# Stored weight sums, one more seven-product group, three listings and a new ending in an eight-core decoder trunk

## The chip, the cores and the metric

One Trainium2 chip; the kernel runs on 8 cores, one sequence of 2048 tokens each, with no traffic between them. The metric is the device time of the slowest core, in microseconds. Some executions are slow: the cores of one die, or a pair of them, run at a lower granted TensorE clock (the share of its full speed that the trace shows as granted): in one run of before, of 2322.42 us, cores 4 to 7 had mean clocks of 0.807 to 0.813, the others 0.987 to 0.993. Runs that count as slow are kept out of all comparisons.

## The reference, cut to what matters

```python
c_act = silu(c)
for l in range(2):                                   # x: (8, 2048, 1024) float32
    mod = c_act @ w_mod[l] + b_mod[l]                # shift, scale, gate of three sub-layers
    h, gate = modulate(x, norm_g[l, 0], mod_f1)      # rmsnorm(x) * (1 + scale) + shift
    x = x + 0.5 * gate * swiglu(h, w_ffn_in[l, 0], w_ffn_out[l, 0])     # hidden width 2816
    h, gate = modulate(x, norm_g[l, 1], mod_mx)
    y = mixer_ab(h, ...) if l == 0 else mixer_pool(h, ...)
    x = x + gate * y
    h, gate = modulate(x, norm_g[l, 2], mod_f2)
    x = x + 0.5 * gate * swiglu(h, w_ffn_in[l, 1], w_ffn_out[l, 1])
return rmsnorm(x, final_g)
```

## The kernel before

Each SwiGLU is done in two passes of two 512-token tiles; I write F10p1 for layer 1, first SwiGLU ("first mixer" in the prediction), second pass. The 2816 hidden channels make 22 blocks: group 0 (12) and group 1 (10). A group is a gate stretch (28 products of 128 x 128 by 128 x 512 per block) and a down stretch. The products are done 2 x 2 with seven instead of eight block products. For that, VectorE forms four sums of a weight piece, and in the down stretch more sums of activations and more updates of X. A group is in `SEVEN` if its down projection is done so too.

```python
SEVEN = {(("F", l, i, p), g) for g in range(2) for l in range(2) for i in range(2) for p in range(2)
         if g == 0 or l == 0 or (l, i, p) == (1, 0, 0)}
KEEP = {}
...
def piece_sums(pc):                       # VectorE, 4 x 128x512 f16 per piece
    tt_(v(4), v(3), v(2), ALU.add, ...);      tt_(v(3), v(0), v(3), ALU.subtract, ...)
    tt_(v(5), v(4), v(0), ALU.subtract, ...); tt_(v(6), v(1), v(5), ALU.subtract, ...)
    if pc.keep is not None:               # there already, used by no piece
        add("sp", dma_start(out=sums_d[pc.keep], in_=SL[:, s, 1536:3584]), ...)
```

Weight pieces come by GpSimd's DMA into six slots (`SLOTS`). The modulation is made of 144 rows of 512 KB: SyncE loads a row into one of two `WMOD` buffers, VectorE multiplies it by the conditioning vector and adds up (1.22 us). Rows are mixed into the stream one at a time when VectorE has less than `SLACK` us of backlog.

```python
SLACK = 3
def slack():
    return Sd.tl["dve"].busy_after(Sd.tl["pe"].tail() - 0.5) < SLACK
def rows_pump():
    ...
    if row_tick[0] >= ROW_EVERY and rows_on[0] and slack():
        q = row_queue.pop(0); row_dot(q); row_prefetch()
def late_x():                             # tiles of the second pass, in F00p0's first down stretch
    for t in range(2, 4):
        for c in range(0, NC, 2):
            add("sp", dma_start(out=X[:, t, c:c + 2, :], in_=xT[t]...), ...)    # 512 KB
            yield
            yield
```

The pooling mixer is mixed into F10p1's group 1 and F11p0. The program is recorded with estimated costs and then "listed": each engine's order is made anew by due times. Orders are fixed when the program is built; every engine then works in its order (in the profile of after VectorE stands 4.07 us at the head of its order while TensorE needs what is behind).

```python
Sd.relist(("dve", "act", "pe"))           # once
...
rstd([3], True)                           # ending: statistic, Ln, Exp, then 8 chunks on VectorE
for c in range(NC):
    final_chunk(3, c)                     # two chunks per store
```

## Time and profile before

| | before |
|---|---|
| runs, us | 1938.27, 1973.97 (slow), 1936.89, 1937.07 |
| cores of the profiled run, us | 1927.7 to 1933.5, median 1930.8 |
| TensorE / VectorE busy, slowest core | 1880.4 / 1694.7 us |
| 20th real product starts | 68.7 us (median core) |
| start of the last product to the end | 13.3 us |

Two groups of VectorE work on the page of before (busy time, mean ns, then idle time ahead of the group and what ended most of it), which the change moves:

```profile
L465 DVE TENSOR_TENSOR SLOTS<-SLOTS 128x512 f16<-128x512 f16 x996 | 395.0, 417 | 17.0 <-DMA SLOTS<-win 10.3
...
L465 DVE SCALAR_TENSOR_TENSOR WMOD<-WMOD,CB 128x1024 f32<-128x1024 f32 x130 | 157.7, 1216 | 7.0 <-DMA WMOD<-wmod 6.9
```

The 996 weight sums cost 395 us of VectorE, and it waits 7 us for rows to land.

### The profile page before, as it was taken

The page shows a single profiled execution, that of the slowest core. Times are in us where ns is not written, and L with a number is a line of the kernel's source. Part 1 is how long each engine was busy: PE and PEld are TensorE (multiplying, and loading weights), DVE is VectorE, ACT ScalarE, POOL GpSimd, SP SyncE. Part 2 cuts the span into 40 slices and gives each one's busy share as a digit, 9 for nine tenths or more (in the row PEclk, how much of TensorE's full clock was granted, in tenths as well). Part 3 has the DMA queues.
Part 4 walks back from the last instruction along what each step waited for, and adds up shares of the span by engine and source line. Part 5 has one row for each costly group of instructions (what it writes and reads, how often), then busy time and mean ns, then how long its engine had stood idle before and what let it go on. Part 6 is the DMA issues. An engine that isn't in the chain of part 4 may idle for free.

```text
span 1933.5 us, 25425 instructions; the slowest of 8 cores (1927.7 to 1933.5 us)
## 1 busy us (share of the span) xinstructions
PE 1880.4 (97%) x8706; PEld 853.4 (44%) x8706; DVE 1694.7 (88%) x3256; ACT 1030.3 (53%) x1738; POOL 174.6 (9%) x330
## 2 busy tenths in 40 slices
PE   3999999999999999999999999999999999999997
PEld 1544444444444444444444444444444444444443
DVE  4897999999988999999988888888998899898865
ACT  3444754456454564555456554654556655664343
POOL 0000000001212000000000000000000000000000
PEclk9899999999999999999999999999999999999999
DMA  9799568797676686867664554555453545445752
GB/s 278 147 174 218 92 119 184 177 190 155 169 177 157 143 190 148 168 137 158 148 119 81 89 87 83 89 96 88 77 88 66 87 77 94 78 74 87 175 86 95
DMA packets 67517, 248.72 MB, mean 129 GB/s; under 512 B 7616, under 2 KB 7744, under 8 KB 67136
## 3 DMA queue, kind: packets, MB, share of 16 engines
q0 software_dynamic: 42192, 153.64, 47.6%
q1 hardware_dynamic: 25200, 93.45, 15.1%
q8 instruction: 74, 1.21, 0.2%
q14 instruction: 51, 0.42, 0.1%
HBM read 392.29 MB, written 8.39 MB: 207 GB/s over the span
## 4 chain that ended last, share of the span: by engine, by line
PE 88%; DMA 4%; DVE 3%; ACT 2%; SPq 1%; issue 1%; POOL 0%; DVEq 0%
PE ps L465 88%; DMA WMOD<-wmod 3%; DMA SLOTS<-win 1%; SPq L465 1%; DVE WMOD L465 1%; DVE SLOTS L465 1%; DVE ACTB L465 1%; DVE TP L465 1%; DVE X L465 0%; ACT ps L465 0%; ACT PMH L465 0%; DVE ps L465 0%; ACT ACTB L465 0%; ACT TP L465 0%; ACT L465 0%
## 5 line engine op out<-in xcount | busy, mean ns | idle before, releaser
L465 PE MATMUL ps<-H,SLOTS 128*128 128x512 f16 x5440 | 1199.7, 379 | 9.3 <-ACT ps L465 3.3
L465 PEld LDWEIGHTS ps<-H,SLOTS 128*128 128x128 f16 x5440 | 530.1, 98 | 657.5 <-issue 28.3
L465 ACT ACTIVATE ps<-ps 128x512 f32<-128x512 f32 x684 | 397.0, 582 | 567.8 <-PE ps L465 529.1
L465 PE MATMUL ps<-ACTB,SLOTS 128*128 128x512 f16 x2780 | 613.8, 379 | 0.1
L465 PEld LDWEIGHTS ps<-ACTB,SLOTS 128*128 128x128 f16 x2780 | 271.8, 98 | 328.4 <-issue 1.4
L465 DVE TENSOR_TENSOR SLOTS<-SLOTS 128x512 f16<-128x512 f16 x996 | 395.0, 417 | 17.0 <-DMA SLOTS<-win 10.3
L465 DVE SCALAR_TENSOR_TENSOR X<-ps,GH,X 128x512 f32<-128x512 f32 x424 | 307.7, 743 | 38.0 <-PE ps L465 34.8
L465 ACT ACTIVATE TP<-ps 128x512 f32<-128x512 f32 x400 | 237.9, 595 | 129.2 <-PE ps L465 126.1
L465 DVE TENSOR_TENSOR ACTB<-TP,ps 128x512 f16<-128x512 f32 x368 | 248.6, 683 | 36.2 <-PE ps L465 22.7
L465 ACT ACTIVATE SQ<-X 128x512 bf16<-128x512 f32 x224 | 131.0, 622 | 111.3 <-DVE X L465 53.6
L465 POOL DMA_DIRECT2D SLOTS<-win x176 | 93.0, 530 | 1032.5 <-PE ps L465 957.8
L465 DVE TENSOR_TENSOR TP<-ps,TP 128x512 f32<-128x512 f32 x176 | 121.0, 687 | 52.4 <-ACT ps L465 50.8
L465 DVE SCALAR_TENSOR_TENSOR WMOD<-WMOD,CB 128x1024 f32<-128x1024 f32 x130 | 157.7, 1216 | 7.0 <-DMA WMOD<-wmod 6.9
L465 DVE TENSOR_TENSOR TP<-X,RS 128x512 f32<-128x512 f32 x192 | 128.8, 686 | 8.1 <-ACT ACTB L465 5.0
L465 DVE TENSOR_TENSOR ps<-ps,TP 128x512 f32<-128x512 f32 x176 | 122.3, 695 | 12.6 <-PE ps L465 10.9
L465 DVE TENSOR_TENSOR ACTB<-ACTB 128x1024 f16<-128x1024 f16 (+1 forms) x188 | 104.3, 565 | 1.4
L465 POOL DMA_DIRECT2D SLOTS<-wout x88 | 46.4, 528 | 502.2 <-PE ps L465 502.2
L465 PE MATMUL ps<-SQ,ONES 128*128 128x512 bf16 x166 | 56.6, 427 | 29.4 <-ACT SQ L465 24.3
L465 ACT ACTIVATE H<-TP,MODT,AS 128x512 f16<-128x512 f32 x81 | 62.5, 805 | 20.3 <-DVE TP L465 13.6
L465 ACT ACTIVATE PMH<-TP,MODT,AS 128x512 f16<-128x512 f32 x60 | 47.5, 805 | 18.9 <-DVE TP L465 18.7
L465 ACT ACTIVATE ACTB<-TP,MODT,AS 128x512 f16<-128x512 f32 x51 | 40.6, 808 | 13.2 <-PE ps L465 7.0
L465 DVE TENSOR_TENSOR SQ<-SQ 128x1024 bf16<-128x1024 bf16 (+1 forms) x56 | 36.2, 647 | 10.5 <-ACT SQ L465 10.1
(74 smaller groups left out, 539.1 us busy)
## 6 DMA issues: line engine op xcount, KB each, us to landing
SLOTS<-win POOLq DMA_DIRECT2D x176, 512.0 KB, 5.7
WMOD<-wmod SPq DMA_DIRECT2D x131, 512.0 KB, 5.9
SLOTS<-wout POOLq DMA_DIRECT2D x88, 512.0 KB, 5.4
SLOTS<-wab POOLq DMA_DIRECT2D x28, 512.0 KB, 8.7
outT<-X SPq DMA_DIRECT2D x16, 512.0 KB, 3.3
ACTB<-wmod SPq DMA_DIRECT2D x13, 512.0 KB, 28.6
X<-xT SPq DMA_DIRECT2D x2, 2048.0 KB, 22.1
X<-xT SPq DMA_DIRECT2D x8, 512.0 KB, 9.7
```

Of the source, the lines that this page charges most:

```text
L465: return lambda E: getattr(E, name)(*a, **k)
```

## The change

The intent: with half of the sums of layer 1's first SwiGLU stored in the first pass and read back in the second, VectorE has room for the seven-product form in F10p1's group 1 as well, which takes 20 products off TensorE. Besides that: three listings, warming products placed as fillers wherever TensorE would be idle in the start, a smaller `SLACK`, and a new ending.

```diff
-WARM = 36
+WARM = 150
+PASSES = 3
-KEEP = {}
-SEVEN = {... or (l, i, p) == (1, 0, 0)}
+KEEP = {(1, 0): lambda g, part, n: n % 2 == 1}
+SEVEN = {... or (l, i, p) in ((1, 0, 0), (1, 0, 1))}
...                                        # listing: fillers have no due time and are dropped
...                                        # after the 20th real product; 51 of 150 remain
-    SLACK = 3
+    SLACK = 2.5
...
-    Sd.BW = 295e3                         # transfer rate assumed in the start
+    Sd.BW = 285e3
...                                        # the last two units: squares not added in pairs
-                    rstd([3], True)
-                    for c in range(NC):
-                        final_chunk(3, c)
+                    rstd([3], True, load=(0.0, 0.0), bank=0)       # Exp into PSUM
+                    act(RS[:, 1, :], PS[0][:], AF.Copy, [("ps", 0)], [("RS", 1)])
+                    for a, b, eng in ((3, 5, "dve"), (0, 2, "pool"), (5, 7, "dve"), (2, 3, "pool"), (7, 8, "dve")):
+                        final_part(3, a, b, eng)                   # VectorE reads PSUM, GpSimd reads RS
...
-    Sd.relist(("dve", "act", "pe"))
+    for _ in range(PASSES):
+        Sd.relist(("dve", "act", "pe"))
```

More of the change, by code (lines that the diff above doesn't have):

```diff
@@ L30, in keeps @@
     return KEEP.get(sub[1:], lambda g, part, n: False)(g, part, n)
-KEEP = {}
-SEVEN = {(("F", l, i, p), g) for g in range(2) for l in range(2) for i in range(2) for p in range(2) if g == 0 or l == 0 or (l, i, p) == (1, 0, 0)}
+KEEP = {(1, 0): lambda g, part, n: n % 2 == 1}
+SEVEN = {(("F", l, i, p), g) for g in range(2) for l in range(2) for i in range(2) for p in range(2) if g == 0 or l == 0 or (l, i, p) in ((1, 0, 0), (1, 0, 1))}
 SLW = 3584
@@ L41 @@
     __slots__ = ("idx", "eng", "fn", "deps", "semkey", "start", "end", "pos", "seq", "signal",
-                 "dma_target", "waits", "clock", "issue", "nbytes", "bw", "after", "then", "gate")
+                 "dma_target", "waits", "clock", "issue", "nbytes", "bw", "after", "then", "gate", "filler")
 class Timeline:
@@ L92, in __init__ @@
         self.wire = Timeline(False)
+        self.fill_to = None
     def key_free(self, k):
@@ L155, in add @@
         op.gate = set()
+        op.filler = 0
         op.start = t
@@ L180, in relist @@
         for o in ops:
-            if o.semkey is None:
+            if o.semkey is None and not o.filler:
                 cost.append(o.end - o.start)
@@ L184, in relist @@
                 cost.append(o.issue)
-            due.append(o.start + (0.0 if o.eng == "pe" else 8.0))
+            due.append(1e9 if o.filler else o.start + (0.0 if o.eng == "pe" else 8.0))
         succ = [[] for _ in ops]
@@ L195, in relist @@
                 left[o.idx] += 1
+                if q.filler:
+                    continue
                 gap = cost[d] if q.semkey is None else cost[d] + 3.5 + q.nbytes / self.BW
@@ L217, in relist @@
         wire = Timeline(False)
+        filling = True
+        stop = [o.idx for o in ops if o.eng == "pe" and self.fill_to is not None and o.idx >= self.fill_to][20:21]
         while events:
@@ L246, in relist @@
                 o.start = t
+                if x in stop:
+                    filling = False
+                if o.filler:
+                    o.filler = 1 if filling else 2
+                    cost[x] = o.issue if filling else 0.0
                 end = t + cost[x]
@@ L270, in emit @@
         by_eng = {e: [] for e in self.ENGS}
-        order = sorted(ops, key=lambda o: (o.start, o.idx))
+        order = sorted((o for o in ops if o.filler < 2), key=lambda o: (o.start, o.idx))
+        live = max((o for o in order if o.filler), key=lambda o: o.start)
         for o in order:
@@ L290, in emit @@
                 q = ops[d]
+                if q.filler == 2:
+                    q = live
                 if q.semkey is not None:
@@ L904, in stats_evac, with rstd @@
         act(RS[:, t % 2, :], PS[st["b"]][:], AF.Copy, [("ps", st["b"])], [("RS", t % 2)])
-    def rstd(ts, direct=False, after=0.0, load=(1.3, 1.3)):
+    def rstd(ts, direct=False, after=0.0, load=(1.3, 1.3), bank=None):
         srcs = {}
@@ L925, in rstd @@
         for i, t in enumerate(ts):
-            chain.append(add("act", I("activation", out=RS[:, t % 2, :], in_=RS[:, t % 2, :], func=AF.Exp, scale=-0.5),
-                             reads=[("RS", t % 2)], writes=[("RS", t % 2)], cost=0.75 + (load[1] if i == n - 1 else 0.0), after=at))
+            out, key = (RS[:, t % 2, :], ("RS", t % 2)) if bank is None else (PS[bank][:], ("ps", bank))
+            chain.append(add("act", I("activation", out=out, in_=RS[:, t % 2, :], func=AF.Exp, scale=-0.5),
+                             reads=[("RS", t % 2)], writes=[key], cost=0.75 + (load[1] if i == n - 1 else 0.0), after=at))
         chain[0].gate = set(table_ops)
@@ L1166, in part @@
                     self.w.done(dch // 2)
-                if self.last and dch % 2 == 1:
+                if self.last and n >= len(self.units) - 2:
+                    while self.sq:
+                        self.sq.pop(0)[0]()
+                    z = sq_rot.next()
+                    act(SQ[:, z, :], Xv(dch, 2 * self.p + tt), AF.Square, [Xk(dch, 2 * self.p + tt)], [("SQ", z)], src="sb")
+                    ones_mm(z, 2 * self.p + tt, NC // 2 + 1)
+                elif self.last and dch % 2 == 1:
                     self.flush_ones(NSQ // 2 - 1)
-                    self.sq.append((squares(dch - 1, 2 * self.p + tt, 2), 2 * self.p + tt))
+                    (q, at), t = squares(dch - 1, 2 * self.p + tt, 2), 2 * self.p + tt
+                    self.sq.append((lambda z=q[0], t=t: ones_mm(z, t, NC // 2 + tt), at))
         def flush_ones(self, most=NSQ // 2):
-            while self.sq and (len(self.sq) > most or self.sq[0][0][1] <= Sd.tl["pe"].tail()):
-                (q, _), t = self.sq.pop(0)
-                ones_mm(q[0], t)
+            while self.sq and (len(self.sq) > most or self.sq[0][1] <= Sd.tl["pe"].tail()):
+                self.sq.pop(0)[0]()
         def segments(self, tail):
@@ L1279, in final_chunk, with final_part @@
                 reads=[Xk(c - 1, t), Xk(c, t)], writes=[("OUT", t, c)], cost=0.06, dma=("OUT", t, c), nbytes=128 * 4096)
+    def final_part(t, a, b, eng):
+        for c in range(a, b):
+            if eng == "dve":
+                stt(Xv(c, t), Xv(c, t), SM[:, SM_FG + c:SM_FG + c + 1], PS[0][:], ALU.mult, ALU.mult,
+                    [Xk(c, t), "SM", ("ps", 0)], [Xk(c, t)])
+            else:
+                act(Xv(c, t), Xv(c, t), AF.Copy, [Xk(c, t), "SM"], [Xk(c, t)], src="sb", scale=SM[:, SM_FG + c:SM_FG + c + 1])
+                add("pool", I("tensor_tensor", out=Xv(c, t), in0=Xv(c, t), in1=RS[:, t % 2, :], op=ALU.mult),
+                    reads=[Xk(c, t), ("RS", t % 2)], writes=[Xk(c, t)], cost=c_pool(TT))
+        add("sp" if eng == "dve" else "act", I("dma_start", out=outT[t][:, a * TT:b * TT], in_=X[:, t, a:b, :]),
+            reads=[Xk(c, t) for c in range(a, b)], writes=[("OUT", t, c) for c in range(a, b)], cost=0.06, dma=("OUT", t, a),
+            nbytes=128 * 2048 * (b - a))
     BS = Af32[:, 40 * 256:42 * 256]
@@ L1575, in build_nc @@
     for n in range(WARM):
-        op = mm(PS[5][:], ONES[:], SQ[:, n % NSQ, :], True, True, [("SQ", n % NSQ), "ONES"], [("ps", 5)])
-        op.after = 28.0 + n * 0.6
-        op.start, op.end = op.after, op.after + op.issue
+        op = add("pe", I("matmul", PS[5][:], ONES[:], SQ[:, n % NSQ, :], start=True, stop=True, skip_group_check=True),
+                 reads=[("SQ", n % NSQ), "ONES"], writes=[("ps", 5)], cost=0.0)
+        op.issue, op.filler = c_pe(TT), 1
     tmp_rot.items = list(range(NTP))
@@ L1603, in build_nc @@
     Sd.BW = Sched.BW
+    Sd.fill_to = len(Sd.ops)
     for ph in PHASES:
@@ L1722, in build_nc @@
                         final_chunk(2, c)
-                    while dn.sq:
-                        (q, _), t = dn.sq.pop(0)
-                        ones_mm(q[0], t)
-                    rstd([3], True)
-                    for c in range(NC):
-                        final_chunk(3, c)
+                    rstd([3], True, load=(0.0, 0.0), bank=0)
+                    act(RS[:, 1, :], PS[0][:], AF.Copy, [("ps", 0)], [("RS", 1)])
+                    for a, b, eng in ((3, 5, "dve"), (0, 2, "pool"), (5, 7, "dve"), (2, 3, "pool"), (7, 8, "dve")):
+                        final_part(3, a, b, eng)
         else:
@@ L1738, in build_nc @@
         marks.append((sub, p, t_begin, Sd.tl["pe"].tail()))
-    add("sp", None, reads=[("OUT", t, c) for t in range(4) for c in (1, 3, 5, 7)], cost=0.01)
-    Sd.relist(("dve", "act", "pe"))
+    add("sp", None, reads=[("OUT", t, c) for t in range(4) for c in ((1, 3, 5, 7) if t < 3 else range(NC))], cost=0.01)
+    for _ in range(PASSES):
+        Sd.relist(("dve", "act", "pe"))
     with nc.Block() as block:
```

## The prediction

> **What bounds the kernel now.** I read the busy row of the page first, then the chain that ended last, then the TensorE timeline with its gaps, then windows of the stage that is changed, and last the beginning and the end of the span.
>
> ```profile
> PE 1880.4 (97%) x8706; PEld 853.4 (44%) x8706; DVE 1694.7 (88%) x3256; ACT 1030.3 (53%) x1738; POOL 174.6 (9%) x330
> PE 88%; DMA 4%; DVE 3%; ACT 2%; SPq 1%; issue 1%; POOL 0%; DVEq 0%
> ...
> 26.36 27.54 DMA WMOD<-wmod
> ...
> 1669.78 250.97 PE ps L465 x1162
> ```
>
> The last line is a stretch of the chain in which TensorE waits for nobody: 250.97 / 1162 = 0.216 us a product. That is the unit of account. The built program issues 8674 TensorE instructions before the change; less the 92 of the start, and less 64 short ones of 128 columns, some 8518 of them at 0.216 us make 1840 us. So about 95 us of the 1933.5 us span are something else: 62 us before the first real product, 13 us after the last one, and about 16 us of gaps and slow clock in between. Only those and the number of products can be gained.
>
> The gaps, from the TensorE timeline, are all small; after 70 us they sum to some 9 us, plus 1.84 us at the very end. The largest, and those in the changed stage:
>
> ```profile
> 188.35 1.02 PE L465 MATMUL ps<-H,SLOTS 128*128 128x512 f16 x4 [1.98 <-DVE TP L465]
> ...
> 1398.93 1.89 PE L465 MATMUL ps<-H,SLOTS 128*128 128x512 f16 x8 [0.24 <-ACT TP L465]
> 1452.33 1.02 PE L465 MATMUL ps<-H,SLOTS 128*128 128x512 f16 x4 [0.76 <-ACT ps L465]
> 1453.66 0.38 PE L465 MATMUL ps<-CB,WMOD 128*128 128x512 f16 x1 [0.31 <-DVE CB L465]
> ```
>
> Counting products places the second pass (p=1) of layer 1's first mixer at about 1281 to 1496 us. Its second hidden group (10 of the 22 blocks) starts near 1397, its plain down projection near 1458. The windows (busy of PE, PEld, DVE, ACT, POOL, then clock, DMA share, GB/s):
>
> ```profile
> 1280.00:1340.00 60.00, 60.00 (x279) 27.20 (x278) 48.97 (x95) 35.22 (x62) 5.29 (x10) 1.00 0.57 97
> 1340.00:1397.00 57.00, 57.00 (x265) 25.82 (x264) 52.75 (x107) 28.03 (x47) 4.57 (x9) 1.00 0.43 75
> 1397.00:1430.00 33.00, 32.76 (x152) 14.72 (x151) 31.57 (x62) 19.19 (x34) 2.81 (x6) 1.00 0.55 96
> 1430.00:1458.00 28.00, 26.77 (x122) 11.45 (x121) 27.76 (x56) 14.61 (x29) 2.11 (x4) 1.00 0.45 76
> 1458.00:1476.00 18.00, 18.00 (x85) 8.17 (x84) 12.46 (x21) 14.29 (x25) 1.59 (x3) 1.00 0.48 75
> 1476.00:1494.00 18.00, 18.00 (x85) 8.17 (x84) 17.88 (x32) 13.12 (x19) 1.06 (x2) 1.00 0.40 70
> ```
>
> From 1397 to 1458 VectorE is busy 59.3 of 61 us: the pooling mixer's vector work runs there beside the weight sums, and TensorE loses 1.3 us. Here VectorE is the second bound. DMA is not: 70 to 97 GB/s, where the first slice of the page shows 278.
>
> [...] after a 3.11 us gap at 45 to 48 us the clock granted from 50 to 60 us is 0.50, with TensorE busy 9.43 of 10. [...]
>
> **The change part by part.** Instruction counts are from the two built programs.
>
> 1. One more seven-product group. Second pass, layer 1, first mixer, group 1: the plain down projection has 16 units of 10 products, 160; the new one 4 x 7 x 5 = 140. Removed: 20 x 0.216 = 4.3 us of TensorE, on the path. It adds for VectorE 8 updates X<-ps,GH,X (24 instead of 16) at 745 ns, 12 activation sums (8 at 687, 4 at 418), and sums of 3 of the 5 output pieces, 12 at 418: 6.0 + 7.2 + 5.0 = 18 us quoted, some 15 us when overlaps are counted (two back to back take 0.75, not 0.84). ScalarE gets 12 copies at 0.58, 7 us; it has room (33.7 of 61).
>
> 2. Half of the sums kept. Odd pieces of all four lists: 6 + 3 of group 0, 5 + 2 of group 1, 16 pieces. 14 of them have sums in the second pass today: 14 x 4 = 56 instructions at 418 ns, 23 us quoted, leave VectorE; 36 in group 0 (13 us net of overlap) and 20 in group 1 (7 us). SyncE gets 16 stores and 16 loads of 512 KB. They add 16.8 MB to 249, and the loads of kept pieces fetch only three quarters of a piece. All of it lies at 1070 to 1496 us where DMA is half idle, 200 us between store and load: nothing on the path.
>
> Sum for this stage. VectorE: 193 busy of 215 us in the pass becomes about 193 - 20 + 15 = 188 of 211, but shifted: group 0 is relieved, group 1 gets 15 - 7 = 8 us more in 93 us, where it had 90 of 97. The order on VectorE shows the weight sums within the pooling stretch falling from 40 to 17, and the stretch behind it, before the next pass's H sums, growing from 57 to 74 instructions, where 5.5 us are idle today. I expect the 1.3 us of waits to go mostly (-1.0) and new short waits in the down projection to give 1.5 back. Stage: -4.3 - 1.0 + 1.5 = -3.8 us.
>
> 3. The start. The 36 fixed warming products become fillers placed wherever the order left TensorE idle; 51 remain. Before, fillers lie between the fp32 row products; now the rows run in one piece with 8 fillers between rows. Row 14 must still wait for its transfer (54.03 us), then row 15's 16 instructions take 3.55 us at half clock. Row 14 loses its interleaved fillers (5 x 0.43 = 2.1 us), but 8 fillers in front of it may hold it up by about 1, and 7 stand before the first real product. [...] I take -1.0, within -4 and +1.
>
> 4. The end:
>
> ```profile
> 1920.78 0.75 DVE L465 SCALAR_TENSOR_TENSOR X<-ps,GH,X 128x512 f32<-128x512 f32 x1 [0.32 <-PE ps L465]
> 1921.56 0.63 ACT L465 ACTIVATE SQ<-X 128x512 bf16<-128x512 f32 x1 [1.10 <-DVE X L465]
> 1922.22 0.42 DVE L465 TENSOR_TENSOR SQ<-SQ 128x512 bf16<-128x512 bf16 x1 [0.69 <-ACT SQ L465]
> ...
> 1923.21 0.69 ACT L465 ACTIVATE RS<-ps,EPSB 128x512 f32<-128x512 f32 x1 [1.02 <-PE ps L465]
> 1923.93 0.63 ACT L465 ACTIVATE RS<-RS 128x512 f32<-128x512 f32 x1
> 1924.59 5.39 DVE L465 SCALAR_TENSOR_TENSOR X<-X,SM,RS 128x512 f32<-128x512 f32 x8 [1.94 <-ACT RS L465]
> ```
>
> After the last update come square, pair sum, statistic, two activations, 8 chunks of 0.67 us and a store that lands 3.5 us later. The change drops the pair sum (0.45), and VectorE makes 5 chunks out of PSUM (about 3.4 us instead of 5.4). ScalarE copies the result (0.6) and GpSimd makes 3 chunks[...]. Last stores are 256 KB. From the update: 2.3 before the pair sum, 1.9 to the second activation's end, 0.6 copy[...] = 10.9, against 1933.5 - 1920.8 = 12.7: -1.8 us.
>
> 5. Three listings instead of one re-order all of TensorE, VectorE and ScalarE. The waits that cost most (table loads of 1.28 us, late rows near 180 us) stay, and the sequences differ in few rows elsewhere. I take -0.5, plus or minus 3.
>
> Sum: -3.8 - 1.0 - 1.8 - 0.5 = -7.1 us. The fast runs of before are 1936.9 and 1938.3; from 1937.6 this makes 1930.5. As listing is made to lessen the waits that remain, I shade it to 1930.
>
> **The rivals.** (a) VectorE becomes the bound in group 1: 98 us of work in 93. For it: 97% busy today and more work on balance. Against: the pooling stretch is what was full, and it is the one relieved. It would eat the 4.3 us: 1934. (b) Stores and loads on SyncE's in-order queue hold up modulation rows or slots: a store waits for VectorE's sums, rows queue behind it, a slot is free only when its store is done. For it: row transfers already hold things up at 180 us. Against: landing takes 5 to 6 us, a slot is held longer, 75 to 97 GB/s. It would cost 3 to 10 us: up to 1938. (c) The three listings remove most of the 9 us of gaps and the start gains 4: 1921. For it: the idle sums are real. Against: they come from delays that the listing doesn't foresee.
>
> **Range and chances.** The parts' errors (2 for the stage, 2 for the start, 3 for the lists, 1 for the end) add to about 4.5 us; 8 in 10 is 1923 to 1936. 2% is 39 us: faster by that would need more than all gaps, the slow clock and the ending together (16 + 13); slower by it, a stall in every pass. I give 0.01 and 0.01.
>
> **What would show it.** Right: 20 fewer ACTB,SLOTS products, 0.216 us each; the gaps at 1399 and 1452 gone; SLOTS sums falling from 996 to 952; the time from last update to end about 11 us; steady TensorE work starting no later than before (69.5 us). Wrong: new gaps before down products near 1460 released by VectorE (rival a); waits on SLOTS<-sums or longer WMOD rows at 1070 to 1490 us (b); fillers standing in front of a row that has landed[...].

The sum of the end came to 10.9 us after the last update, against 12.7, so -1.8: two of its terms are cut, GpSimd's three chunks, which were to end after VectorE's and so set the end, and the last store. The three that stand, 2.3 + 1.9 + 0.6, make 4.8 us. The forecast is -7.1 us in all, 1930.5 us, shaded to 1930.

## The result, and the profile after

| | before | after |
|---|---|---|
| runs, us | 1938.27, 1936.89, 1937.07 | 1933.84, 1933.57, 1931.71, 1937.72 |
| ratio of fast runs | | 0.9983 (0.9963 to 1.0004) |
| median core / slowest, profiled run | 1930.8 / 1933.5 | 1924.7 / 1932.2 |

A ratio is the mean time of one kernel's fast runs over that of the other's of the same rounds, so not quite the ratio of the medians. The point of 1930.0 was missed by 3.7 us, the range of 1923 to 1936 held the median of 1933.7 and three of the four runs. The interval of the ratio reaches over 1, so the 3.2 us between the mean times (1937.4 and 1934.2) are not clear of noise. The stages below are another matter: most of them agree within 0.03 us over the cores of a run, and where they don't the text says why.

The page of after, its busy row and the two VectorE groups:

```profile
PE 1881.2 (97%) x8702; PEld 853.2 (44%) x8702; DVE 1687.4 (87%) x3228; ACT 1035.1 (54%) x1754; POOL 176.7 (9%) x333
...
L480 DVE TENSOR_TENSOR SLOTS<-SLOTS 128x512 f16<-128x512 f16 x952 | 376.1, 418 | 12.6 <-DMA SLOTS<-win 7.6
...
L480 DVE SCALAR_TENSOR_TENSOR WMOD<-WMOD,CB 128x1024 f32<-128x1024 f32 x130 | 158.3, 1218 | 12.7 <-DMA WMOD<-wmod 12.7
```

The sums fell to 952 as predicted, and the wait for rows grew from 7.0 to 12.7 us on this core.

Where did the time go? I counted the products with weights in TensorE's timeline on each core and cut the span where the product of a fixed count starts (from the 6300th on the counts of kernels with the new group are 20 lower). The table has the median over the eight cores of each stage's length, so the rows don't add up exactly.

| stage | products | before | after |
|---|---|---|---|
| start | to 20 | 68.74 | 69.95 |
| F00p0 | 20 to 500 | 104.57 | 103.73 |
| F00p0 | 500 to 560 | 14.87 (max 18.6) | 16.72 (max 21.4) |
| F00p0 | 560 to 924 | 79.67 | 78.76 |
| F00p1 | 924 to 1848 | 201.74 | 201.22 |
| AB mixer, F01 | to 4592 | 604.8 | 604.8 |
| F10p0 | to 5516 | 202.47 | 201.34 |
| F10p1 group 0 | to 6020 | 112.23 | 112.24 |
| F10p1 group 1, gate | to 6300 | 68.34 | 67.77 |
| F10p1 group 1, down | to 6460 | 35.83 | 30.73 |
| F11p0 group 0 | to 6964 | 112.23 | 114.76 |
| F11p0 group 1 | to 7404 | 103.19 | 101.88 |
| F11p1 | to the last | 206.77 | 206.99 |
| last product to the end | | 13.26 | 12.97 |

The last product starts 5.7 us earlier on the median core (1917.4, then 1911.7). Three things stand out: the named group gains 5.7 us, the group behind it gives 2.5 back, and the slowest core gains far less than the median one. Windows of these three stages on the slowest core, first of before (core 3), then of after (core 7); columns as in the prediction:

```profile
1394.00:1462.33 68.33, 66.86 (x307) 29.49 (x306) 66.22 (x132) 39.05 (x71) 5.43 (x11) 1.00 0.47 80
1462.33:1498.17 35.84, 35.84 (x168) 16.26 (x167) 30.61 (x53) 25.34 (x39) 2.50 (x5) 1.00 0.45 74
1498.17:1610.40 112.23, 112.23 (x522) 50.87 (x521) 98.97 (x187) 60.57 (x104) 9.49 (x18) 1.00 0.49 83
```

```profile
1397.19:1464.96 67.77, 67.13 (x312) 30.17 (x311) 66.39 (x124) 43.05 (x79) 5.80 (x11) 1.00 0.55 111
1464.96:1495.69 30.73, 30.73 (x143) 13.80 (x142) 30.20 (x56) 23.20 (x37) 2.12 (x4) 1.00 0.39 70
1495.69:1610.45 114.76, 113.01 (x522) 50.57 (x520) 105.29 (x201) 64.05 (x109) 9.49 (x18) 1.00 0.49 84
```

In the two windows of group 1 TensorE is busy 102.70 us before and 97.86 after, and idle 1.47 and 0.64. But VectorE, which had 5.2 us free in the down stretch, is now busy 30.20 of its 30.73 us and takes a backlog into the next pass: 201 instructions instead of 187 there, and TensorE waits at its head. The gaps of TensorE in the timeline of after, core 7 (start, length, instructions; in brackets the idle time before them and what ended it):

```profile
1498.15 0.38 PE L480 MATMUL ps<-H,SLOTS 128*128 128x512 f16 x1 [0.35 <-ACT ps L480]
1500.83 2.67 PE L480 MATMUL ps<-H,SLOTS 128*128 128x512 f16 x10 [0.79 <-DVE H L480]
1504.05 1.02 PE L480 MATMUL ps<-H,SLOTS 128*128 128x512 f16 x4 [0.54 <-ACT ps L480]
```

These 1.68 us are most of the 2.5 given back. The gaps that the prediction showed at 1399 and 1452 us are gone.

Most of the spread of the cores comes from one place, products 500 to 560. The timeline of after, core 7, VectorE and TensorE:

```profile
190.47 1.23 DVE L480 SCALAR_TENSOR_TENSOR WMOD<-WMOD,CB 128x1024 f32<-128x1024 f32 x1 [4.07 <-DMA WMOD<-wmod]
...
192.45 3.69 PE L480 MATMUL ps<-H,SLOTS 128*128 128x512 f16 x8 [3.97 <-DVE TP L480]
```

VectorE stands 4.07 us at the head of its order, waiting for a modulation row that the AB mixer needs over 250 us later; behind it is what TensorE needs now. In this stage core 7 took 21.4 us, core 1 14.7. Of the 7.5 us by which core 7 stood over the median core, 4.7 come from here, 1.8 from F10p0 and 1.5 from the start. In F10p0 its VectorE waits for a row again, soon after SyncE issued two stores of sums, and TensorE loses 1.58 us behind it:

```profile
1097.76 1.23 DVE L480 SCALAR_TENSOR_TENSOR WMOD<-WMOD,CB 128x1024 f32<-128x1024 f32 x1 [2.99 <-DMA WMOD<-wmod]
```

Without stores, in before and in e2, F10p0 takes 202.46 to 202.48 us on every core; with them some 201.2 where no row is late, up to 203.13 in after and 206.88 in e1. So the late rows here come with the stores; no run tests that by itself. The slowest core stood 7.5, 4.9, 5.1 and 7.9 us over the median core in the four runs of after (6.3 on average), 2.7 in the profiled run of before and 2.3 to 6.8 in 22 other fast runs (4.7 on average).

### The profile page after: what moved, and what is told of

Its sections match the earlier page's. It is cut to its first block, busy times and chain, and to the rows that moved or that the text cites. A ratio compares the mean times of both kernels' runs of the same rounds, so it can differ in the third digit from the quotient of the medians.

```text
span 1932.2 us, 25507 instructions; the slowest of 8 cores (1921.1 to 1932.2 us)
## 1 busy us (share of the span) xinstructions
PE 1881.2 (97%) x8702; PEld 853.2 (44%) x8702; DVE 1687.4 (87%) x3228; ACT 1035.1 (54%) x1754; POOL 176.7 (9%) x333
## 4 chain that ended last, share of the span: by engine, by line
PE 91%; DMA 4%; DVE 2%; SPq 1%; ACT 1%; issue 0%
PE ps L480 91%; DMA WMOD<-wmod 4%; SPq L480 1%; DVE X L480 1%; DVE TP L480 0%; DVE WMOD L480 0%; DVE ACTB L480 0%; DVE SLOTS L480 0%; ACT SQ L480 0%; ACT ps L480 0%; ACT L480 0%; ACT H L480 0%; ACT TP L480 0%; ACT PMH L480 0%; ACT ACTB L480 0%
## 5 line engine op out<-in xcount | busy, mean ns | idle before, releaser
L480 ACT ACTIVATE ps<-ps 128x512 f32<-128x512 f32 x696 | 404.5, 582 | 585.1 <-PE ps L480 575.0
L480 DVE TENSOR_TENSOR SLOTS<-SLOTS 128x512 f16<-128x512 f16 x952 | 376.1, 418 | 12.6 <-DMA SLOTS<-win 7.6
L480 DVE SCALAR_TENSOR_TENSOR X<-ps,GH,X 128x512 f32<-128x512 f32 x432 | 312.8, 746 | 30.9 <-PE ps L480 26.1
L480 DVE SCALAR_TENSOR_TENSOR WMOD<-WMOD,CB 128x1024 f32<-128x1024 f32 x130 | 158.3, 1218 | 12.7 <-DMA WMOD<-wmod 12.7
L480 DVE TENSOR_TENSOR ACTB<-ACTB 128x1024 f16<-128x1024 f16 (+1 forms) x200 | 111.3, 567 | 1.2
L480 DVE TENSOR_TENSOR H<-H 128x1024 f16<-128x1024 f16 (+1 forms) x72 | 43.6, 624 | 2.1 <-ACT H L480 2.0
```

Of the source, the lines that this page charges most:

```text
L480: return lambda E: getattr(E, name)(*a, **k)
```

## The experiments

Twelve kernels ran, e1 to e12; all were correct. When I wrote the expectations I took the stage bounds wrongly from the counts: products 4976 to 5900 are called the first pass or F10p0 in them, and 5900 to 7000 "the stage". Really 5900 to 7000 is the end of F10p1's group 0, its group 1 and all of F11p0's group 0. The counts and the lengths are as stated, so the tests hold; this table has both, the true stages first (medians of eight cores, us).

| | before | after | e1 | e2 | e3 | e4 | e9 | e10 |
|---|---|---|---|---|---|---|---|---|
| F10p0 | 202.47 | 201.34 | 201.16 | 202.47 | 201.16 | 201.15 | 201.30 | 205.53 |
| F10p1 g1 gate | 68.34 | 67.77 | 71.76 | 64.55 | 67.34 | 69.37 | 71.15 | 67.34 |
| F10p1 g1 down | 35.83 | 30.73 | 35.96 | 41.21 | 34.53 | 36.24 | 30.22 | 30.22 |
| F11p0 g0 | 112.23 | 114.76 | 113.20 | 118.58 | 112.43 | 113.20 | 114.96 | 113.83 |
| F11p0 g1 | 103.19 | 101.88 | 103.20 | 101.88 | 101.88 | 101.87 | 103.30 | 101.88 |
| products 5900 to 6200 | 70.33 | 70.20 | 73.32 | 69.07 | 69.93 | 70.14 | 70.37 | 70.36 |
| products 6200 to 7000 | 182.33 | 179.32 | 183.87 | 191.64 | 180.64 | 184.93 | 183.79 | 177.28 |
| last product starts | 1917.4 | 1911.7 | 1919.9 | 1924.3 | 1914.8 | 1919.3 | 1918.9 | 1914.2 |

### e1_keepseven: the two named parts alone

```diff
-KEEP = {}                                 (in the kernel before)
+KEEP = {(1, 0): lambda g, part, n: n % 2 == 1}
-... or (l, i, p) == (1, 0, 0)}
+... or (l, i, p) in ((1, 0, 0), (1, 0, 1))}
```

> The kernel before with only the kept sums and the extra seven-product group; start, listing and ending as before. Stages are counted in products with the weight slots, per core. My theory (the stated change is worth its 20 products and the waits of that stage): from product 6200 to 7000 (20 fewer) 182.3 us becomes about 179.3, as in the changed kernel; the stages next to it (the first pass of this mixer, 202.5; products 7000 to 7924, 208.5) stay, as do the start (product 20 at 68.7) and the ending; the median core is 3 us shorter, ratio 0.998. Rival (the listings make the gain): 6200 to 7000 stays within 1 us of 182.3. Rival (stores and loads cost): the first pass, where stores are, grows above 202.5.

Measured: 1942.48 us, ratio 1.0013 (0.9995 to 1.0031). The three stages from F10p1's group 1 to F11p0's group 0 take 220.92 us, 216.40 before: 4.5 us longer with 20 products less; products 6200 to 7000 take 183.87 us, where I had expected 179.3. In the timeline of its slowest core TensorE waits four times in the down stretch, 5.1 us in all, like this:

```profile
1492.13 1.24 PE L465 MATMUL ps<-ACTB,SLOTS 128*128 128x512 f16 x5 [1.46 <-DVE X L465]
...
1498.95 3.40 PE L465 MATMUL ps<-ACTB,SLOTS 128*128 128x512 f16 x15 [1.86 <-ACT ps L465]
```

So the named parts alone, in the old listing, cost more in waits on VectorE than they save.

### e2_nokeep: after, without stored sums

```diff
-KEEP = {(1, 0): lambda g, part, n: n % 2 == 1}
+KEEP = {}
```

> The changed kernel with nothing kept: the second pass makes all its sums again, 64 more on VectorE, and there is no store or reload. If VectorE is the second bound there (my theory), products 6200 to 7000 take 181 to 185 us instead of 179.3, with gaps released by VectorE, and the kernel is 2 to 5 us slower than the changed one. If the kept sums only unload an engine that has room, 179.3 stays and the time with it. If the reloads cost something, this kernel is faster.

Measured: 1947.3 us, ratio 1.0036 (1.0018 to 1.0054). The three stages take 224.34 us, 11.1 more than in after (213.26), and VectorE is busy 41.20 of the 41.21 us of the down stretch. I had expected 181 to 185 us for products 6200 to 7000, and they take 191.64. The stored sums are what makes the group pay. They also shorten F10p0: 202.47 without, 201.15 to 201.34 with them in e1, e3, e4 and after; the two gaps of 0.32 and 0.67 us before 1200 us stand in e2 as in before.

### e3_noseven: after, without the new group

```diff
-... or (l, i, p) in ((1, 0, 0), (1, 0, 1))}
+... or (l, i, p) == (1, 0, 0)}
```

> The changed kernel with the old set of seven-product groups; sums are kept. My theory: products 6200 to 7000 (again 20 more) take 179.3 + 4.3, less the waits that come with the extra group (about 1.5): 182 to 183; the kernel is 2.5 to 4 us slower than the changed one. Rival (the group's gain is eaten by VectorE and the relief by kept sums gives the 3 us): 180 to 181 and the time equal within 1 us.

Measured: 1936.81 and 1933.43 us in two fast runs, two slow, so no ratio; the profile is of a fast run. The three stages take 214.30 us, against 213.26 with the group: it is worth 1.04 us, not 4.3. With plain products TensorE doesn't wait once in these stages on the slowest core; with seven it loses what the table shows at F11p0's head. Products 6200 to 7000 took 180.64 us; the rival's 180 to 181 was right, mine of 182 to 183 wrong.

### e4_onepass: after, listed once

```diff
-PASSES = 3
+PASSES = 1
```

> The changed kernel listed once instead of three times. If the listings made the gains outside the named stage, products 4976 to 5900 go back from 201.2 to 202.5, products 7000 to 7924 from 207.2 to 208.5, 560 to 700 from 30.4 to 31.3, and the median core is 3 to 4 us longer. If they come from the kept sums, the fillers or the smaller slack, these stages stay at 201.2, 207.2 and 30.4. The spread of the cores at products 500 to 560 should tell whether the order of the third listing or chance makes the late rows worse: 14.7 to 18 us here if it is the order, up to 21 as in the changed kernel if not.

Measured: 1939.42 us, ratio 1.0001 (0.9985 to 1.0017). The last product starts 7.6 us later than in after. The three stages take 218.81 us (5.6 more), F01p0 203.24 (201.73), the rest hardly changes. F10p0 stays at 201.15, where I had expected the listings to have made the gain; they didn't, the stored sums did (e2). Products 500 to 560 take up to 21.4 us here too, so it is not the order of the third listing that makes the rows late.

### e5_warm37: after, fewer fillers offered

```diff
-WARM = 150
+WARM = 37
```

> The changed kernel with 37 fillers instead of 150 offered: the 14 that stood behind row 15, in front of and among the first real products, are gone; those before the rows stay. My theory (fillers in front delay the first products, and with them the copy on ScalarE behind which the last H chunks wait): from the end of row 15 to product 20 it takes 9.3 us in the changed kernel and 6.8 before; here 6.5 to 7.5, product 20 at 67 to 68.5 instead of 70.0, and the whole kernel 1.5 to 2.5 us shorter on the median core. Rival (the last H chunks and their sums set the start anyway): product 100 stays at 87.3 within 0.5 and the time with it.

Measured: 1931.08 us, ratio 1.0001 (0.9948 to 1.0053); of its four runs one (1952.67) has a pair of cores at a granted clock of 0.971, and counts as fast; the other three are 1928.8 to 1932.9. The 20th product starts at 68.54 us (69.95 in after), as expected, and product 100 earlier too, so the rival is out. The median core of the profiled run ends at 1924.7 us, as in after, so the 1.5 to 2.5 us are not seen there; over the three undisturbed runs it ends at 1921.7 to 1924.7, in the four of after at 1924.7 to 1928.3. TensorE's timeline, after core 7, then e5 core 6:

```profile
61.78 3.15 PE L480 MATMUL ps<-SQ,ONES 128*128 128x512 bf16 x7
64.72 1.76 PE L480 MATMUL ps<-H,SLOTS 128*128 128x512 f16 x4
66.32 0.38 PE L480 MATMUL ps<-SQ,ONES 128*128 128x512 bf16 x1
```

```profile
61.27 0.59 PE L480 MATMUL ps<-SQ,ONES 128*128 128x512 bf16 x1 [0.40 <-DVE AS L480]
61.65 5.33 PE L480 MATMUL ps<-H,SLOTS 128*128 128x512 f16 x17
```

In after, seven fillers, at half clock still (0.50 granted from 61.78 to 64.72 us), stand in front of the first real product, and nine more among the next; in e5 one is left in front, and 17 products run in one piece behind it. From the end of row 15 to the first real product it takes 2.80 us in after, 0.78 in e5 and 0.24 in before, on every core.

### e6_hold: after, rows 24 to 31 held back and made up in group 1 of F00p0

```diff
+        held = 24 <= q < 32               # in row_dma: not before TensorE's work at this point
+            op.deps.add(max(o.idx for o in Sd.ops[-120:] if o.eng == "pe"))
-            if row_queue:
+            if row_queue and row_queue[0] < row_cap[0]:       # 24, lifted in group 1, rows on there
```

> The changed kernel with modulation rows 24 to 31, which are needed only by the next mixer, held back until the late X tiles are in. My theory (these rows land late behind the X tiles, VectorE waits for them in its order, and TensorE behind it; the slowest core of a run is the one hit hardest): products 500 to 560 take 14.7 to 15.5 us on every core instead of 14.7 to 21.4, the slowest core comes within 3 us of the median core instead of 5 to 8, and the kernel is 3 to 5 us faster than the changed one, about 1929 to 1930. Rival (weight pieces that land late do it): the spread at 500 to 560 stays above 3 us. Rival (the spread comes from elsewhere): 500 to 560 is even, the slowest core stays 5 us over the median.

Measured: three fast runs of 1933.25 to 1936.14 us, ratio 0.9987 (0.9972 to 1.0003). Products 500 to 560 take 14.7 to 15.4 us on all cores, and the slowest core stands 2.1 us over the median one in the profiled run (3.3 and 5.3 in the other two): the cause of this stage's spread is as thought, but not all of the cores' spread lies in this stage. And 560 to 924 grows from 78.76 to 83.91: the rows that were held now stand in the way of the next group. No net gain.

### e7_tail: after, a second Exp for the copy and smaller first pieces

```diff
-                    act(RS[:, 1, :], PS[0][:], AF.Copy, [("ps", 0)], [("RS", 1)])
-   ((3, 5, "dve"), (0, 2, "pool"), (5, 7, "dve"), (2, 3, "pool"), (7, 8, "dve"))
+                    act(RS[:, 1, :], RS[:, 1, :], AF.Exp, [("RS", 1)], [("RS", 1)], src="sb", scale=-0.5)
+   ((3, 4, "dve"), (0, 1, "pool"), (4, 6, "dve"), (1, 3, "pool"), (6, 8, "dve"))
```

> The changed kernel with the second activation made twice, into PSUM and into SBUF, so that VectorE need not wait for the copy, and with first pieces of one chunk. My theory (the end is the first store plus 2.1 MB at some 400 GB/s): VectorE starts its chunks 0.6 us after the first of the two activations ends instead of 1.2, the first store is ready 1.2 us sooner, and the time from the last product to the end falls from 13.0 to about 11.8 us. Rival (GpSimd's chunks set the end, as I predicted): it stays at 12.4 or more.

Measured: two fast runs, 1931.29 and 1930.37 us, ratio 0.9969 (0.9951 to 0.9987); last product to end 12.06 us instead of 12.97. The timelines of the ending, after core 7, then e7 core 0:

```profile
1922.42 0.60 ACT L480 ACTIVATE ps<-RS 128x512 f32<-128x512 f32 x1
1923.05 0.60 ACT L480 ACTIVATE RS<-ps 128x512 f32<-128x512 f32 x1
1923.68 3.88 DVE L480 SCALAR_TENSOR_TENSOR X<-X,SM,ps 128x512 f32<-128x512 f32 x5 [3.21 <-ACT RS L480]
1923.73 3.72 POOL L480 TENSOR_TENSOR X<-X,RS 128x512 f32<-128x512 f32 x3 [41.83 <-ACT RS L480]
```

```profile
1921.37 0.63 ACT L480 ACTIVATE RS<-RS 128x512 f32<-128x512 f32 x1
1921.37 3.88 DVE L480 SCALAR_TENSOR_TENSOR X<-X,SM,ps 128x512 f32<-128x512 f32 x5 [2.58 <-ACT ps L480]
1922.08 3.71 POOL L480 TENSOR_TENSOR X<-X,RS 128x512 f32<-128x512 f32 x3 [41.86 <-ACT RS L480]
```

In after VectorE waits for the copy as well (the copy ends at 1923.65 us, VectorE starts at 1923.68): both read the same PSUM bank, and the program orders the two readers; no run here tried without. With a second Exp from SBUF, VectorE starts as soon as the first is done (at 1921.37 us in e7, where the first ends at 1921.33). VectorE's five chunks take 3.88 us in both kernels, though GpSimd starts 0.05 us behind VectorE in after and 0.71 us behind it in e7: no slowing of VectorE by GpSimd shows here. The rest of after is bound by the stores: a window of its core 7 holds nothing but transfers.

```profile
1928.00:1930.00 2.00, 0.00 (x0) 0.00 (x0) 0.00 (x0) 0.00 (x0) 0.00 (x0) 0.50 1.02 401
```

In e7 it is no longer the stores alone. Its first store is issued 4.6 us after the last product starts, 6.0 in after: that is 1.4 us earlier, but the end comes only 0.9 earlier. Between the first pieces its DMA engines are partly idle, 0.70 busy from 1923 to 1924 us, and then (core 0):

```profile
1924.00:1925.00 1.00, 0.00 (x0) 0.00 (x0) 0.96 (x2) 0.00 (x0) 1.00 (x2) 0.50 0.74 281
```

So there the chunks hold the stores up again. What each of the two edits is worth alone no run shows.

### e8_hold6: after, six rows held until F00p1

```diff
-    row_cap = [24]                        (of e6)
+    row_cap = [26]                        # lifted at F00p1's start, no rows in group 1
```

> The hold again, on six rows alone (26 to 31, which were the ones that VectorE met while their loads stood behind the eight token tiles), let go at the start of the first mixer's second pass, and with no rows made up in the group between. Theory (the spread of the slowest core comes from VectorE waiting in order for rows that nobody needs yet): products 500 to 560 take 14.7 to 16 us on every core, products 700 to 924 take 48.35 again and not the 53.5 of the first hold, the slowest core stands at most 3.5 us over the median core, and the slowest core's span is 1925 to 1929 where the changed kernel had 1932.2. Rival (the spread is the cores' own, and only moves to another stage): slowest less median stays at 5 to 8 us with the excess in another stage, and the time stays at 1931 to 1934.

Measured: 1968.68 to 1980.93 us, ratio 1.0185 (1.0154 to 1.0216), "unclear" by the rule; all four runs count as fast, but have cores at a lower clock, so this ratio is not one of undisturbed runs. The stall is gone as expected (median 14.92; two cores at a lower clock took 17.8), and 560 to 924 is back at 78.74. But F00p1 takes 203.97 us and the first 80 products of the AB mixer 29.1 to 35.0 us, by core, instead of 17.3: the rows had become due, and the mixer waited. My expectation had VectorE's missing 7 us vanish in F00p1; VectorE has no such room. What follows on some cores is worse. Windows of e8, core 0 and then core 6:

```profile
500.00:550.00 50.00, 50.00 (x216) 21.90 (x215) 34.56 (x64) 15.39 (x27) 7.49 (x16) 0.81 0.57 123
```

```profile
70.00:150.00 80.00, 80.00 (x306) 33.10 (x305) 63.24 (x128) 31.94 (x56) 5.30 (x10) 0.81 0.58 115
```

After the pause core 0 (as 1, 2 and 3) was granted 0.81 of the clock from 500 to 650 us, core 5 all of it. Cores at a mean clock of 0.962 to 0.979 stand in all four runs of e8. That the pause sets this off is not shown: cores 6 and 7 of the same run, 6 the slowest of all, had 0.81 from 70 us on, long before it, and most kernels had such runs.

### e9_slack3: after, with the old SLACK

```diff
-    SLACK = 2.5
+    SLACK = 3
```

> The changed kernel with the one figure SLACK back at 3, with three listings. Theory (the small gains far from the named stage are SLACK's, since one listing kept most of them): products 560 to 700 take 31.1 to 31.3 us (30.41 with 2.5), products 7000 to 7924 take 208.2 to 208.5 (207.20), the first mixer's second pass 201.5 to 201.7 (201.22), in sum +1.5 to +2.6 us. Rival (the other start or the listings make them): these three stay within 0.2 us of the changed kernel's.

Measured: one run, 1939.63 us. Half a miss: 560 to 924 (78.74) and F00p1 (201.27) don't change, so that gain isn't SLACK's; F11p0's group 1 goes back to 103.30 as I thought. But the largest effect lies where I had not looked for it: F10p1's gate stretch takes 71.15 us (67.77), and the last product starts 7.2 us later. With the old SLACK the three named stages take 216.32 to 219.68 us, by core, median 217.89: they gain nothing on before (216.40).

### e10_keepall: after, all 33 eligible sums stored

```diff
-KEEP = {(1, 0): lambda g, part, n: n % 2 == 1}
+KEEP = {(1, 0): lambda g, part, n: True}
```

> All 33 eligible sums stored and reloaded instead of 16: 68 fewer sums of 0.39 us, about 27 us less of VectorE, in the second pass. Theory (with seven products in group 1 VectorE is what the stage waits for, and gave back 3.3 of the 4.3 us): the stage falls from 249.5 to 246 to 247 us, the first pass stays at 201.2, the median core ends 2.5 to 3.5 us earlier, 1921 to 1922. Rival (17 more stores and reloads of 0.5 MB meet SyncE's row loads or the weight loads): the first pass grows by over 1 us or the stage stays at 249 or over, with waits of TensorE or VectorE on DMA in either.

Measured: 1936.4 to 1937.1 us in three runs; a fourth, 1959.73, has a pair of cores at 0.979 but counts as fast, and the ratio of 1.0026 (0.9964 to 1.0088) is with it. The median core ends at 1927.5, not at 1921 to 1922. Both theories are half right. The three stages fall to 211.39 us (213.26), with group 1 at 97.56, free of waits: VectorE was the bound. But F10p0 grows by 4.2 us. The waits in F10p0, slowest core:

```profile
POOL SLOTS L480 <- DMA sums<-SLOTS: 54.3, 9, 15.8
```

GpSimd's order waits nine times for stores to land before it may refill a slot; its DMA engines are busy 0.94 of this stage at 217 GB/s (0.78 and 171 GB/s on core 7 of after, where no such wait is listed). That is the prediction's rival (b), which half as many stores escape in this form; the late rows of F10p0 above are another.

### e11_all3: after, with the mends of e5, e7 and e8

> The changed kernel with three mends together: 37 fillers offered, the six rows held, the second Exp and one-chunk first pieces at the end. Theory (they lie in different stages and add): the start -1.4, the tail -0.9, so the median core at 1922 to 1923 (1924.7 in the changed kernel) and the slowest within 3.5 us of it: 1924 to 1927, a ratio to the kernel before of 0.993 to 0.995. Rival (a wait in one of the later stages takes up what the earlier ones free): 1929 to 1932.

Measured: 1940.62 us at best. Of five runs that count as fast two are undisturbed (1940.62 and 1945.88) and three have a pair of cores at 0.970 to 0.979; the ratio of 1.015 (1.0128 to 1.0172) is over all five. The 20th product starts at 67.13 and the tail takes 12.33 us, as expected, but e8's loss comes with it. Windows of core 0 at the head of the AB mixer:

```profile
460.00:470.00 10.00, 7.85 (x36) 3.23 (x35) 10.00 (x19) 5.24 (x8) 0.00 (x0) 1.00 0.48 148
...
480.00:490.00 10.00, 7.39 (x22) 2.29 (x22) 4.63 (x9) 5.84 (x10) 0.34 (x2) 0.61 1.01 172
```

VectorE is full while TensorE begins to wait, then the mixer's first steps wait for each other. In after the first AB pass takes 100.21 us, here 112.90.

### e12_spread: after, with the mends of e5 and e7, and the tile loads spread instead of the rows held

```diff
+    def every(side, first, step):         # hand on one load every `step` segments
+                    run_segs(segs[:-3], every(xs, 24, 9) if k == 0 else iter(()))    # gate stretch
-                    run_down(dn, rest, late_x() if k == 0 else iter(()))
+                    run_down(dn, rest, every(xs, 2, 2) if k == 0 else iter(()))
```

> The three mends once more, but with the rows left where they were: the eight loads of the first pair of token tiles, which stand close together in the first down stretch, are spread from the middle of the gate stretch on, so that the rows' loads meet no full DMA engines and no VectorE work moves to a later stage; 37 fillers and the mended ending as before. Theory (the stall at products 500 to 560 is a burst of 4.2 MB of tile loads in about 20 us on top of weights and rows): products 500 to 560 take 14.7 to 16 us on every core, 700 to 924 stays at 48.35, the first mixer's second pass at 201.2 to 201.7 and the two passes after it at 285.1, the slowest core stands at most 4.5 us over the median one; with the start at 68.5 and the tail at 12.1 the median core ends at 1922 to 1924 and the slowest at 1924.5 to 1928, a ratio of 0.994 to 0.997. Rival (the rows or the first down stretch now wait for the tiles, earlier): a wait of over 2 us on DMA between products 100 and 500 on most cores, and the slowest core at 1930 or over.

(The eight loads are in fact those of the second pair of tiles, 2 and 3.) Measured: three undisturbed runs of 1925.46, 1926.74 and 1927.14 us; three slow; and one of 1951.07 that counts as fast but has its cores 6 and 7 at clocks of 0.973 and 0.979 and 1944.9 and 1949.3 us. The ratio, with that run, is 0.9985 (0.9907 to 1.0062). Worked out without it, the three runs over the seven undisturbed ones of before in the same call (1934.98 to 1939.54) give 1926.45 / 1937.37 = 0.9944, and the two sets don't overlap. In the profile, products 500 to 560 take 14.24 to 14.26 us on every core, the AB mixer 100.21 a pass, the 20th product starts at 67.90, the tail takes 12.15; the median core ends at 1920.5, the slowest at 1924.9. In the three undisturbed runs the slowest core stands 4.4, 2.8 and 5.0 us over the median one, so some spread from elsewhere is left. The rival's wait on tiles didn't come (20 to 500 takes 104.02 us, 0.3 more). Windows at the place of the stall, after core 7 and then e12 core 7:

```profile
180.00:190.00 10.00, 7.93 (x36) 3.46 (x36) 4.59 (x9) 7.80 (x15) 1.18 (x3) 1.00 1.02 209
```

```profile
180.00:190.00 10.00, 10.00 (x48) 4.53 (x47) 8.94 (x19) 7.40 (x13) 1.05 (x2) 1.00 0.82 199
```

On this core the DMA engines are no longer full (0.82 of the window instead of 1.02), TensorE is busy for all of it instead of 7.93 us, and no VectorE work was moved. On core 0 of e12 they are still full in this window (1.03), but 0.67 busy in the 10 us before, where core 7 of after has 1.04; VectorE waits for rows 4.7 us in all from 70 to 1900 us there, 11.6 us on core 7 of after. That the spread loads end the stall, e12 shows; that they do so by leaving the DMA engines room for the rows fits these numbers, but no run tests it by itself.

## Why the prediction was right or wrong

The total was right within its range, and only partly for its reasons: it foresaw -7.1 us, the profiled median core gained 6.1, and the time 3.2 (mean of the fast runs, 1937.4 and 1934.2). That the sum came out near is luck: the group with the stored sums, the start and the end were to give 6.6 us and gave 2.2, and stages that the prediction did not name gave 4.6 (point 4). The profiled run of after is also its best by the median core. Over its four runs the median core ends at 1926.3 us on average, over 22 fast runs of before at 1931.4, which makes 5.2 us.

1. **The group and the stored sums: -3.8 predicted, -3.1 measured** (216.40 to 213.26). The 20 products came off at 0.216 us and the old waits mostly went (1.31 us, then 0.64), as written. "New short waits in the down projection to give 1.5 back" was too small and in the wrong place: the down stretch has none, the backlog of VectorE is paid at the head of the next pass, 2.5 us. And the agreement is luck in part. With one listing and the old SLACK the same two parts lose 4.5 us (e1), with three listings and the old SLACK they gain nothing (e9), with one listing and the new SLACK they lose 2.4 (e4). The prediction left SLACK out altogether.

2. **Start: -1.0 predicted, +1.2 measured.** The clean rows are worth what was said: from the start of row 14 to the end of row 15 it takes 6.68 us instead of 7.92 (medians of the cores). The step that failed is the weight given to the fillers: those in front of the first product and among the next ones cost more than the clean rows saved. From the end of row 15 to the 20th product it takes 9.60 us instead of 6.79 (7.57 in e5, which is 1.4 us faster in the whole start).

3. **End: -1.8 predicted, -0.3 measured.** The pair sum went, and VectorE reads PSUM as worked out. Two terms were missing: VectorE waits for the copy too, 0.63 us (e7), and the last tile's 2.1 MB of stores run at about 400 GB/s, which makes some 5.2 us of transfers (an estimate from the two), and in after these end last. VectorE's five chunks took 3.88 us (0.78 each; 3.4 was predicted from 0.67 each). GpSimd's three took 3.72 us (1.24 each), and end before VectorE's, at 1927.45 us against 1927.56; the prediction had them end last. The prediction's own sum is off as well: on its lines the time from the update to the pair sum is 1.44 us (1920.78 to 1922.22), not 2.3, so its terms make 10.0 us, not 10.9, and the miss of the end is larger by 0.9.

4. **Listings: -0.5 predicted.** This was the most mis-sized term: three instead of one are worth 7.6 us on the median core (e4), 5.6 of them in the named stages and 1.5 in F01p0, part of which only undoes what the other parts disturb. Outside the named stages after gained 0.8, 0.9, 0.5, 1.1 and 1.3 us. The 1.1 are the stored sums' (e2), the 1.3 are SLACK's (e9). The 0.5 of F00p1 is within what its cores differ by (e1 has it as well). The 0.8 and 0.9 of F00p0 are missing in e1 and stay, wholly or mostly, when SLACK goes back (e9), the program is listed once (e4) or the fillers are fewer (e5, for the 0.9); whether the fillers as such or the assumed rate of the start make them stays open.

5. **The row wait near 180 us** was said to "stay". Its size differs by core and run, 0 to 6.7 us in the profile of after, and the slowest core is the metric. The slowest core stood 6.3 us over the median one on average, 4.7 in before: that is why some 5 us on the median core became 3.2 in the time. Why it grew is open: in its median the stage takes 14.87 us in before and in e1, 16.71 in after, but e1's worst core took 21.3 as well. e6 shows what makes this stage long (hold the rows and it is 14.7 to 15.4 us everywhere), e8 and e11 that VectorE's work can't be put off in this way, e12 that the burst of tile loads can be thinned out.

Of the rivals, (a) is true in part: three of the 4.3 us are eaten (e3), 2.3 of them behind group 1; (b) appears in after as rows that are late in F10p0 on some cores (2.99 us on core 7), one of the signs that the prediction named for it, and as slots held up with twice the stores (e10); (c) saw the size of the listings, but not that others would eat it.

## What to carry to other kernels

Taking products off the busiest engine paid here only what the second-busiest left, 1.04 of 4.3 us (e3): test it by taking the product saving away again and reading the stage and the one behind it. On several cores, look at every core's stage times: what varies by core is paid at its worst (products 500 to 560 took 14.7 us on core 1 of after, 21.4 on core 7, the slowest). When an engine that works in its order waits for data that isn't needed yet, thin out the burst of loads ahead of the data (14.24 to 14.26 us on every core in e12) before you put off the work: the work that was put off here fell due later (560 to 924 grew to 83.91 us in e6, F00p1 to 203.97 in e8).
